# A mixture-of-experts layer on one core: another order of the 32 experts, and one norm of the last stage issued one tile later

## The chip, the core and the metric

The kernel runs on one core of one Trainium2 chip. Times are device microseconds (us) of that core for one whole launch. A core has TensorE (PE, matmuls and transposes; its weight loads are listed as PEld), VectorE (DVE), ScalarE (ACT), GpSimd (POOL) and SyncE (SP, which here only issues DMAs). Each engine works through its own queue in order, and they wait for one another by semaphores.

## The reference

One decoder layer on 1024 tokens of 1024 columns: a mixer (pooling and dilated attention), then a mixture of experts, a gated per-layer embedding and a final norm. What matters here:

```
h = rmsnorm(x);  logits = h @ w_router + b_router          # 32 experts, top 4 of each token
for each expert e, over the tokens that chose it:
    g, u = split(h @ w_gate_up[e] + b_gate_up[e])          # 1024 -> 2 x 1024
    a = (clip(u) + 1) * min(g, 7) * sigmoid(1.702 * min(g, 7))
    x[token] += gate * (a @ w_down[e] + b_down[e])
x += (p @ w_ple_proj) * sigmoid(rmsnorm(x) @ w_ple_gate)   # last stage, p: 1024 x 256
out = rmsnorm(x)
```

All of it is float32. The order in which the experts are taken is free.

## The kernel before, in words

**Exact products.** A float32 operand is split into a high and a low part (`split`, L103 to L105): ACT copies the high part (L104, tiles `wh`, `xh`, `ah`, `xr`), DVE subtracts it from the source (L105, `wl`, `xl`, `al`, `atr`). A product is then three matmuls (`mm3`, L98 to L101). Each half of a weight chunk of 128 x 2048 goes through this: one ACT instruction, then one DVE instruction.

**Places.** The experts are sorted by how many rows they have. The 18 largest (`N_MORE`, ranks 0 to 17) get 128 main rows and 32 *further* rows, the other 14 get 128. `processing_order` (L39) says which rank stands at which of the 32 places, `RANK` keeps it, and `REM[s]` is 1 where the expert at place `s` has further rows. This is a table made before the launch: it decides the order of instructions on every engine. Written as a string of `REM`, the table before is `01010101101010110101010110101011`.

**Main loop** (from L1177). The chunks are g(0), g(1), d(0), g(2), d(1), ... , g(31), d(30), d(31): g(s) is gate/up of place s (8 chunks), d(s) its down product (4 chunks). SP loads chunks six ahead into 7 tiles `raw`; ACT and DVE split them two chunks ahead of PE (`split_half`). The row groups below count a *window* from the first bias matmul of g(s) (L1029) to that of g(s+1); it holds g(s) and d(s-1). Beside the chunks a window has: the swiglu (`act_all`), the transposes of the result (`a_main`, L1007), the transposes of the next expert's rows (`x_main`), the row lists of place s+2 (`onehots`, `lists`) and, on POOL, gathers of rows (L934) and adds of results to `acc` in device memory (L1118).

**Further rows.** Where `REM[s]` is 1: `gu_rem` (L1043) puts 32 matmuls (L1057) after chunk k = 1 and 32 after k = 5 of g(s); `act_rem` is a small swiglu at k = 6; `x_rem(s)` (L1024, tile `xr`) transposes the gathered further rows during g(s-1), after its chunk k = 5 (PE L1019, then an ACT copy L1021); `a_rem` transposes the result (tile `atr`), `down_rem` (L1107) puts 64 matmuls (L1114) after chunk 1 of d(s) (after chunk 0 at the last place), and `y_rem` scales and adds (L1130, L1118).

**Last stage.** `proj(i)` (L1329), i = 0 to 7, multiplies tile i of p; its operand is transposed and split two tiles ahead (`turn_p`, L1170, PE L1174, ACT and DVE into `xr` and `atr`), and the products are copied out by ACT (L1336) and DVE (L1337). Into these eight steps the first norms of the stage are put: `early(n)` (L1390) squares tile n of the residual on ACT (L1346) and has nine small DVE instructions (`small_rsqrt`, L131 to L141) and one big one (L1349). `TURN0` (L1138) gives the values of i after which `early(0)` and `early(1)` are issued. Before `proj(7)` PE transposes the result of `early(0)` (`turn(0)`, L1007). Then come eight tiles of gate product, sigmoid, norm and store.

Of the kernel before, what the change touches and what calls it, by code (L numbers as in the profile page):

```python
# [26 lines left out]
NE = 32  # L27
# [7 lines left out]
N_MORE = 18  # L35
# [2 lines left out]

def processing_order():  # L39
    more, less = list(range(N_MORE)), list(range(N_MORE, NE))  # L40
    return [(more if (s + 1) * N_MORE // NE > s * N_MORE // NE else less).pop(0) for s in range(NE)]


RANK = processing_order()
REM = [int(r < N_MORE) for r in RANK]

# [25 lines left out]
def layer(ctx, tc, x, p, g_mix, w_in, w_pool, pool_scale, rel_bias, w_out, g_ffn, w_router,  # L72
# [170 lines left out]
    for i in range(NT):  # L243
# [13 lines left out]
        if i == 4:  # L257
            m = qk0.tile([128, 4, T], F32R, name="qk0")
            m = [m[:, 0], m[:, 1]]
# [257 lines left out]
    for u in range(32 + LAG + 2):  # L517
# [9 lines left out]
        if u == MIX:  # L527
            m = tbp.tile([128, 2, NK, 128], F32R, name="tb", bufs=1)
# [364 lines left out]
    def load_chunk(c, after=None, columns=slice(0, 2048)):  # L893
        kind, s, k = chunks[c]
        if c not in raws:
            raws[c] = wp.tile([128, 2048], F32, name="raw", bufs=7)
        if after is not None:
            after.memset(raws[c][:, columns][:, :1], 0.0)
        if kind in "jp":
            src = w_ple_gate[k * 256:(k + 1) * 256, :] if kind == "p" else w_ple_proj  # L900
            sp.dma_start(raws[c].rearrange("p (k c) -> p k c", k=2), src.rearrange("(k p) c -> p k c", p=128))
            return
        if s not in expert:
            expert[s] = sp.value_load(order[0:1, s:s + 1], min_val=0, max_val=NE - 1)
        e = expert[s]
        if kind == "g":
            sp.dma_start(raws[c][:, columns],
                         w_gate_up[ds(e, 1), k * 128:(k + 1) * 128, columns].rearrange("a p c -> p (a c)"))
        else:
            sp.dma_start(raws[c].rearrange("p (k c) -> p k c", k=2),  # L910
                         w_down[ds(e, 1), k * 256:(k + 1) * 256, :].rearrange("a (k p) c -> p (a k) c", p=128))
# [223 lines left out]
        y_rem(s)  # L1135
        S[s].clear()

    LOADS, SPLITS, TURN0, AT = 6, 4, (3, 7), 8  # L1138
    load_chunk(0, columns=slice(1024, 2048))

    lists(0, gates=False)
# [35 lines left out]
    for c, (kind, s, k) in enumerate(chunks[:nmain]):  # L1177
# [7 lines left out]
        if kind == "g":  # L1185
# [19 lines left out]
            if s == 0 and k == GK:  # L1205
                m = psM.tile([128, 2, 2, 6], F32, name="m", bufs=1)
# [241 lines left out]
```

## Time and profile before

| | |
|---|---|
| median of 3 runs | 1970.8 us (1970.47 to 1974.77) |
| profiled execution, its own time | 1971.62 us |
| its span, first to last instruction | 1969.8 us |
| PE busy | 1920.4 us (97%) |
| DVE, ACT, POOL busy | 1501.4, 1187.4, 282.0 us |
| main loop and last stage | from about 465 us to the end |

The busy time of PE counts a matmul from its start to its modelled end, and matmuls overlap: a matmul of 512 columns is shown with 0.39 us, but one starts every 0.227 us. So the loss of PE is read from the distance of two starts, or from the length of a window, not from the busy share.

### The profile page before, as it was taken

The page shows a single profiled execution, that of the slowest core. Times are in us where ns is not written, and L with a number is a line of the kernel's source. Part 1 is how long each engine was busy: PE and PEld are TensorE (multiplying, and loading weights), DVE is VectorE, ACT ScalarE, POOL GpSimd, SP SyncE. Part 2 cuts the span into 40 slices and gives each one's busy share as a digit, 9 for nine tenths or more (in the row PEclk, how much of TensorE's full clock was granted, in tenths as well). Part 3 has the DMA queues.
Part 4 walks back from the last instruction along what each step waited for, and adds up shares of the span by engine and source line. Part 5 has one row for each costly group of instructions (what it writes and reads, how often), then busy time and mean ns, then how long its engine had stood idle before and what let it go on. Part 6 is the DMA issues. An engine that isn't in the chain of part 4 may idle for free. (4 is left out here: it accounts for less than half of the span.)

```text
span 1969.8 us, 30297 instructions
## 1 busy us (share of the span) xinstructions
PE 1920.4 (97%) x11180; PEld 1428.8 (73%) x11181; DVE 1501.4 (76%) x2500; ACT 1187.4 (60%) x1706; POOL 282.0 (14%) x219
## 2 busy tenths in 40 slices
PE   7999999997999999999999999999999999999998
PEld 6778767775677776677776677776766777766786
DVE  5342575768889897888897888897977898978676
ACT  4221565445667676676676666776766676765533
POOL 0000121002122020212021212120202120201100
PEclk9999999997999999999999999999999999999999
DMA  4331212428889798798897798897987897987611
GB/s 150 115 93 38 87 45 65 137 110 316 345 319 354 282 378 306 285 345 340 310 363 283 294 349 328 311 360 279 359 322 291 317 353 283 377 308 275 205 65 54
DMA packets 117369, 502.18 MB, mean 255 GB/s; under 512 B 12560, under 2 KB 28944, under 8 KB 84576
## 3 DMA queue, kind: packets, MB, share of 16 engines
q1 hardware_dynamic: 99920, 451.46, 58.6%
q0 software_dynamic: 12960, 39.33, 8.5%
q10 hardware_dynamic: 4336, 9.40, 1.5%
q8 instruction: 89, 1.46, 0.3%
q14 instruction: 64, 0.52, 0.1%
HBM read 466.04 MB, written 38.83 MB: 256 GB/s over the span
## 5 line engine op out<-in xcount | busy, mean ns | idle before, releaser
L105 DVE TENSOR_TENSOR wl<-raw,wh 128x1024 fp32r<-128x1024 f32 x778 | 902.7, 1221 | 89.9 <-ACT wh L104 85.3
L104 ACT ACTIVATE wh<-raw 128x1024 fp32r<-128x1024 f32 x778 | 758.5, 1059 | 1.6 <-DMA raw<-in_w_gate_up 1.1
L99 PE MATMUL gu<-wh,xh 128*128 128x512 f32 x1152 | 487.3, 423 | 0.0
L100 PE MATMUL gu<-wl,xh 128*128 128x512 f32 x1152 | 449.7, 390 | 1.4 <-DVE wl L105 1.4
L101 PE MATMUL gu<-wh,xl 128*128 128x512 f32 x1152 | 449.9, 391 | 0.0
L99 PEld LDWEIGHTS gu<-wh,xh 128*128 128x128 f32 x1152 | 218.5, 190 | 47.8 <-issue 12.8
L101 PEld LDWEIGHTS gu<-wh,xl 128*128 128x128 f32 x1152 | 216.6, 188 | 46.5
L100 PEld LDWEIGHTS gu<-wl,xh 128*128 128x128 f32 x1152 | 217.7, 189 | 41.4 <-DVE wl L105 2.6
L100 PE MATMUL d<-wl,ah 128*128 128x512 f32 x512 | 199.9, 390 | 2.9 <-DVE wl L105 2.9
L99 PE MATMUL d<-wh,ah 128*128 128x512 f32 x512 | 201.6, 394 | 0.7 <-DVE al L105 0.7
L101 PE MATMUL d<-wh,al 128*128 128x512 f32 x512 | 199.2, 389 | 0.0
L1118 POOL DMA_INDIRECT acc<-y,idx x32 | 128.6, 4017 | 441.3 <-ACT y L1124 324.0
L934 POOL DMA_INDIRECT xg<-h2d,idx x32 | 52.7, 1645 | 671.4 <-PE gu L100 471.3
L1057 PE MATMUL r<-raw,xr 128*32 128x512 f32 x1152 | 130.5, 594 | 0.0
L1124 ACT ACTIVATE y<-d,gate 128x512 f32<-128x512 f32 x64 | 43.7, 689 | 127.1 <-PE d L101 122.4
L104 ACT ACTIVATE ah<-d 128x512 fp32r<-128x512 f32 x64 | 34.8, 596 | 139.4 <-PE d L1007 139.4
L105 DVE TENSOR_TENSOR al<-d,ah 128x512 fp32r<-128x512 f32 x64 | 41.2, 686 | 99.5 <-ACT ah L104 99.5
L99 PEld LDWEIGHTS d<-wh,ah 128*128 128x128 f32 x512 | 96.1, 188 | 27.8 <-ACT wh L104 7.0
L100 PEld LDWEIGHTS d<-wl,ah 128*128 128x128 f32 x512 | 96.1, 188 | 23.6 <-DVE wl L105 4.6
L101 PEld LDWEIGHTS d<-wh,al 128*128 128x128 f32 x512 | 96.1, 188 | 20.1
L104 ACT ACTIVATE xh<-d 128x512 fp32r<-128x512 f32 x80 | 43.7, 597 | 84.1 <-PE d L1007 84.1
L1057 PEld LDWEIGHTS r<-raw,xr 128*32 128x32 f32 x1152 | 34.2, 109 | 73.7 <-issue 72.1
(362 smaller groups left out, 2518.3 us busy)
## 6 DMA issues: line engine op xcount, KB each, us to landing
raw<-in_w_gate_up SPq DMA_DIRECT2D x255, 1024.0 KB, 5.8
raw<-in_w_down SPq DMA_DIRECT2D x128, 1024.0 KB, 5.4
wr<-in_w_in SPq DMA_DIRECT2D x16, 512.0 KB, 6.3
rrep<-rvec ACTq DMA_DIRECT2D x8, 576.0 KB, 13.9
xt<-in_x SPq DMA_DIRECT2D x8, 512.0 KB, 3.6
tb<-rrep SPq DMA_DIRECT2D x8, 512.0 KB, 6.1
wor<-in_w_out SPq DMA_DIRECT2D x8, 512.0 KB, 3.8
xr<-in_x SPq DMA_DIRECT2D x8, 512.0 KB
```

The costliest lines, as they stand in the source:

```text
L99: pe.matmul(ps, wh, xh, start=start, stop=False)
L100: pe.matmul(ps, wh, xl, start=False, stop=False)
L101: pe.matmul(ps, wl, xh, start=False, stop=stop)
L104: act.activation(hi, src, AF.Copy)
L105: dve.tensor_tensor(lo, src, hi.bitcast(F32), OP.subtract)
L934: pool.indirect_dma_start(out=xg, out_offset=None, in_=h2d4 if b else h2d, in_offset=bass.IndirectOffsetOnAxis(ap=S[s]["idx", b][:, :1], a ...
L1057: pe.matmul(S[s]["gur"][32 * j:32 * j + 32, :], S[s]["xr"][:, kk, :], raw[:, :, j, :], start=False, stop=(kk == NK - 1))
L1118: pool.indirect_dma_start(out=dst, out_offset=bass.IndirectOffsetOnAxis(ap=idx[:, :1], axis=0), in_=src, in_offset=None, compute_op=OP.add)
L1124: act.activation(y[:, 512 * b:512 * b + 512], S[s]["d"][b], AF.Copy, scale=S[s]["gate", 0])
```

## The change

The places are filled in another way: the first and the last place get an expert without further rows, and the 18 with further rows are spread over the 30 places between. The table is now `01010110101101011010110101101010`. Both tables have 18 ones and no two zeros side by side; they differ in the places where two ones meet: before at 7/8, 14/15, 23/24 and 30/31, now at 5/6, 10/11, 15/16, 20/21 and 25/26. The first place had no further rows before either. The second edit puts `early(0)` after `proj(4)` instead of `proj(3)`. Three lines more make every later line number larger by 3.

```diff
 def processing_order():
     more, less = list(range(N_MORE)), list(range(N_MORE, NE))
-    return [(more if (s + 1) * N_MORE // NE > s * N_MORE // NE else less).pop(0) for s in range(NE)]
+
+    n = NE - 2
+    many = [False] + [(s * N_MORE + n // 2) // n > ((s - 1) * N_MORE + n // 2) // n for s in range(1, n + 1)] + [False]
+    return [(more if m else less).pop(0) for m in many]
...
-    LOADS, SPLITS, TURN0, AT = 6, 4, (3, 7), 8
+    LOADS, SPLITS, TURN0, AT = 6, 4, (4, 7), 8
```

ACT in g(5), before: after the splits of the next expert's rows (`xh`) there are weight splits (`wh`), the small swiglu of place 5 (`uc`, `sg` from `r`) and the big one (from `gu`).

```order
L104 ACTIVATE xh<-d_6622 128x512
L104 ACTIVATE xh<-d_6629 128x512
L104 ACTIVATE wh<-raw 128x1024 x4
L1067 ACTIVATE uc_6706<-r 128x256
L1068 ACTIVATE sg<-r 128x256
L104 ACTIVATE wh<-raw 128x1024 x2
L1067 ACTIVATE uc_6773<-gu_6464 128x512
```

The same stretch of ACT now:

```order
L107 ACTIVATE xh<-d_6641 128x512
L107 ACTIVATE xh<-d_6648 128x512
L107 ACTIVATE wh<-raw 128x1024 x2
L1024 ACTIVATE xr<-m 128x2x4x32
L107 ACTIVATE wh<-raw 128x1024 x2
L1070 ACTIVATE uc_6730<-r 128x256
L1071 ACTIVATE sg<-r 128x256
L107 ACTIVATE wh<-raw 128x1024 x2
L1070 ACTIVATE uc_6778<-gu_6483 128x512
```

Place 6 now has further rows, so the copy of their transposes (`xr<-m`) stands in front of two weight splits and of the swiglu. Before, such a copy stood inside the window of an expert with further rows at places 7, 14, 23 and 30.

PE around the start of d(31), the down product of the last place, before: the last matmul of d(30), the transposes of the swiglu's result (`uc512`), those of the further rows (`uc256`), and the first matmuls of d(31).

```order
L101 MATMUL d1_17730<-wh_17749,al_17530 128x512
L1007 MATMUL d0_17853<-ident_62,uc512_17706 128x128 x4
L1007 MATMUL d1_17860<-ident_62,uc512_17710 128x128 x4
L1019 MATMUL m_17867<-ident_62,uc256_17677 128x128 x2
L99 MATMUL d0_17882<-wh_17800,ah_17851 128x512
L100 MATMUL d0_17882<-wl_17801,ah_17851 128x512
```

The same place on PE now:

```order
L104 MATMUL d1_17771<-wh_17790,al_17594 128x512
L1010 MATMUL d0_17894<-ident_62,uc512_17747 128x128 x4
L1010 MATMUL d1_17901<-ident_62,uc512_17751 128x128 x4
L102 MATMUL d0_17918<-wh_17841,ah_17892 128x512
L103 MATMUL d0_17918<-wl_17842,ah_17892 128x512
```

The two transposes of the further rows are gone from here, and so are the 64 matmuls (L1114) that stood after the first chunk of d(31); both kinds now stand in windows of earlier places.

DVE between `proj(3)` and `proj(5)`, before: the end of `early(0)` (`nr`, `y`), then the low part of tile 6 of p (`atr`), the copy out of `proj(4)`, a weight split, and the low part of tile 7.

```order
L141 SCALAR_TENSOR_TENSOR nr_18380<-na_18382,nr_18380 128x1
L1349 SCALAR_TENSOR_TENSOR y_18375<-xg_18260,nr_18380,oh_18257 128x1024
L105 TENSOR_TENSOR atr_18404<-m_18405,xr_18403 128x256
L1337 COPY raw_18390<-gu1_18254 128x512
L105 TENSOR_TENSOR wl_18413<-raw_17932,wh_18412 128x1024
L105 TENSOR_TENSOR atr_18429<-r_18430,xr_18428 128x256
```

DVE now: the low part of tile 6 (`atr_18388`), the copy and the split come first, and then `early(0)` begins.

```order
L108 TENSOR_TENSOR atr_18388<-m_18389,xr_18387 128x256
L1340 COPY raw_18374<-gu1_18254 128x512
L108 TENSOR_TENSOR wl_18397<-raw_17932,wh_18396 128x1024
L1396 TENSOR_SCALAR ss2_18400<-ss2_18400 128x1
L134 TENSOR_SCALAR nn_18404<-ss2_18400 128x1
L136 TENSOR_SCALAR nr_18406<-nn_18404 128x1
```

The whole of `early(0)` moved behind three instructions; it now stands ahead of the low part of tile 7 instead of tile 6.

## Rows read from the trace of the kernel before

**Rows 1.** The page: busy time of PE, and TensorE's clock in 40 slices.
```profile
PE 1920.4 (97%) x11180; PEld 1428.8 (73%) x11181; DVE 1501.4 (76%) x2500; ACT 1187.4 (60%) x1706; POOL 282.0 (14%) x219
...
PEclk9999999997999999999999999999999999999999
```

**Rows 2.** Waits of PE: line, releaser, us in total, times, longest.
```profile
PE d L100 <- DVE wl L105: 2.9, 4, 0.8
...
PE gu L101 <- DVE atr L105: 0.7, 1, 0.7
PE d L99 <- DVE al L105: 0.7, 1, 0.7
```

**Rows 3.** Windows of places 5 to 9: length, then busy time of each engine, PEclk, DMA.
```profile
663.54:707.22 43.68, 43.68 (x250) 30.87 (x250) 34.81 (x54) 29.46 (x38) 6.24 (x4) 1.00 0.85 313
707.22:747.52 40.30, 40.30 (x250) 31.35 (x250) 38.03 (x54) 29.10 (x37) 10.19 (x3) 1.00 0.90 350
747.52:792.23 44.71, 43.96 (x243) 30.76 (x243) 33.64 (x48) 29.52 (x39) 4.46 (x3) 1.00 0.84 316
792.23:839.98 47.75, 47.75 (x316) 32.91 (x316) 39.55 (x58) 29.48 (x38) 10.44 (x3) 1.00 0.77 282
839.98:880.10 40.12, 40.12 (x242) 31.16 (x242) 35.10 (x47) 29.47 (x38) 4.46 (x3) 1.00 0.91 345
```

**Rows 4.** Timeline of PE in d(6) and d(29): start us, us, instruction [idle before].
```profile
785.72 0.39 PE L99 MATMUL d<-wh,ah 128*128 128x512 f32 x1
786.86 0.50 PE L100 MATMUL d<-wl,ah 128*128 128x512 f32 x1 [0.75 <-DVE wl L105]
...
1770.20 0.39 PE L99 MATMUL d<-wh,ah 128*128 128x512 f32 x1
1771.22 0.50 PE L100 MATMUL d<-wl,ah 128*128 128x512 f32 x1 [0.62 <-DVE wl L105]
```

**Rows 5.** Timeline of ACT in the window of place 7.
```profile
774.69 0.39 ACT L1021 ACTIVATE xr<-m 128x256 f32<-128x256 f32 x1 [4.13 <-PE m L1019]
...
781.25 7.70 ACT L104 ACTIVATE wh<-raw 128x1024 fp32r<-128x1024 f32 x8
```

**Rows 6.** Timeline of DVE in the same window.
```profile
785.59 4.63 DVE L105 TENSOR_TENSOR wl<-raw,wh 128x1024 fp32r<-128x1024 f32 x4
```

**Rows 7.** Timeline of PE at the start of d(31).
```profile
1824.30 0.38 PE L1019 MATMUL m<-ident,uc 128*128 128x128 f32 x2
1825.38 0.50 PE L99 MATMUL d<-wh,ah 128*128 128x512 f32 x1 [0.70 <-DVE al L105]
...
1828.01 0.39 PE L101 MATMUL d<-wh,al 128*128 128x512 f32 x1
...
1831.91 0.50 PE L99 MATMUL d<-wh,ah 128*128 128x512 f32 x1
```

**Rows 8.** Timeline of PE in `proj(6)` and at `turn(0)`.
```profile
1859.56 0.39 PE L100 MATMUL gu<-wl,xr 128*128 128x512 f32 x1
1860.70 0.50 PE L101 MATMUL gu<-wh,atr 128*128 128x512 f32 x1 [0.75 <-DVE atr L105]
...
1863.10 1.04 PE L1007 MATMUL d<-ident,y 128*128 128x128 f32 x8
```

**Rows 9.** Timeline of ACT around `early(0)` and `proj(4)`.
```profile
1855.73 1.06 ACT L1346 ACTIVATE y<-xg 128x1024 f32<-128x1024 f32 x1 [0.37 <-issue]
...
1857.53 1.06 ACT L104 ACTIVATE wh<-raw 128x1024 fp32r<-128x1024 f32 x1
```

**Rows 10.** Timeline of DVE in `early(0)`: its first and last instruction, and the next.
```profile
1856.92 0.15 DVE L1393 TENSOR_SCALAR ss<-ss 128x1 f32<-128x1 f32 x1 [0.30 <-ACT y L1346]
...
1859.02 1.29 DVE L1349 SCALAR_TENSOR_TENSOR y<-xg,nr,oh 128x1024 f32<-128x1024 f32 x1 [0.22 <-DVE nr L141]
1860.22 0.42 DVE L105 TENSOR_TENSOR atr<-m,xr 128x256 fp32r<-128x256 f32 x1
```

**Rows 11.** A stretch before the main loop, columns as in rows 3.
```profile
447.50:468.00 20.50, 13.44 (x68) 8.71 (x67) 14.51 (x56) 10.24 (x19) 2.18 (x8) 0.50 0.62 227
```

## The prediction, made before the changed kernel was run

> **What bounds the kernel now.** I read the page's busy rows first: PE is busy 97% of the span, and its clock row stands near full throughout [rows 1]. A busy share proves little, since overlapping matmuls are counted whole, so I went to the list of PE's waits next. It is short: from the main loop on, the entries are 2.9 us in four waits for `wl`, 0.7 us in one for `al` and 0.7 us in one for `atr` [rows 2]; nothing there waits for a weight load. Then I cut the main loop into windows from one expert's first bias matmul to the next one's. The reader should see that a window's length depends only on who has further rows, and that PE's busy time equals the length except in one of the five [rows 3]. So the order cannot make the stream shorter; both orders have the same number of matmuls. It can only add or remove gaps of PE, and move work into or out of gaps. The sum below counts these.
>
> **The windows by kind.** Write a window as (place before, own place, next place, the one after). The trace shows (0,1,0,1) at 43.68 us, (1,0,1,1) at 40.30, (0,1,1,0) at 44.71, (1,1,0,1) at 47.75 and (1,0,1,0) at 40.12 [rows 3]; all the other windows of places 2 to 29 repeat one of these within 0.02 us. Before, places 2 to 29 hold 9 windows of 43.68, 9 of 40.12, 4 of 40.30, 3 of 44.71 and 3 of 47.75: 393.12 + 361.08 + 161.20 + 134.13 + 143.25 = 1192.8 us. With the new table they hold 6, 7, 5, 5 and 5: 262.08 + 280.84 + 201.50 + 223.55 + 238.75 = 1206.7 us, which is 13.9 more. Every window of the new table is of a kind that the trace has, with the same neighbours two places to either side. This is why I trust the sum.
>
> **What leaves the end in return.** At the last place an expert with further rows is replaced by one without. Three pieces go.
> - In the window of place 30: the two transposes of place 31's further rows and the gap described below. An (0,1,1,0) window is 44.71 against 43.68 of (0,1,0,1), which is 1.03; the fourth gap is 0.13 shorter than the others and a list of place s+2 with further rows costs 0.18 (40.30 less 40.12), so I put this at 1.06.
> - In the window of place 31: its further gate/up matmuls. From 47.75 less 40.12, corrected by the same 0.18 and by the 0.30 for the transposes (1.03 + 0.18 - 0.91), that is 7.75.
> - In d(31): the 64 further matmuls, from the matmul at 1828.01 to the one at 1831.91 less one step of 0.23: 3.67 [rows 7].
>
> The loop's sum is +13.9 - 1.06 - 7.75 - 3.67 = **+1.4 us**, slower. Two causes stand behind it, and they can be priced alone:
>
> 1. *One more pair.* Where an expert with further rows is followed by another, PE has a gap: from 785.72 to 786.86 is 1.14 us against a step of 0.23, so 0.91 is lost; in the fourth such pair it is 1.02, so 0.79 [rows 4]. The chain behind it: in g(7) ACT must copy the transposes of place 8's further rows, but PE reaches them only after the 32 further matmuls of place 7, and ACT sits idle 4.13 us [rows 5]. That eats its lead; the swiglu follows, the next weight splits start at 781.25 [rows 5], and DVE's `wl` starts at 785.59 [rows 6], just too late. Where only one of the neighbours has further rows the window has no such gap. There were 4 pairs, there are 5: 5 x 0.91 - (3 x 0.91 + 0.79) = +1.03.
> 2. *A cover lost.* At the start of d(31) PE waits for `al` in any case [rows 2, 7]. The two transposes of the last expert's further rows (1824.30) ran inside this wait; now all eighteen such pairs run in the full stream. The full cost of further down rows in a window is 47.75 - 43.68 = 4.07, at the last place 3.67: +0.4.
>
> Bounds for the pairs: below, no gap at any pair in the new spacing, -3.5 instead of +1.0; above, twice the gap in each pair after the first. I take the measured gap, since three of four agree to 0.01 us.
>
> **The norm, one tile later.** Before, `early(0)` holds DVE from 1856.92 to 1860.31, and the low part of tile 6 stands behind it [rows 10]; PE waits for that part in `proj(6)`: 1859.56 to 1860.70 is 1.14, so 0.91 lost [rows 8]. With `early(0)` behind the copy and the split of `proj(4)` this gap goes. What is late next is `turn(0)`, which needs the norm's result. ACT's last work in `proj(4)` is the split at 1857.53, ending at 1858.59 with the squares in front of it and up to 0.3 earlier without [rows 9]. From the start of the squares to DVE's first instruction of the norm it is 1.19 (1855.73 to 1856.92) [rows 9, 10], plus at most the 0.37 of idle time that stood ahead of the squares: DVE begins between 1859.5 and 1860.1. The DVE work of the norm takes 3.39 (1856.92 to 1860.31) [rows 10], so the result is there between 1862.9 and 1863.5, and `turn(0)` starts some 0.06 later. Before, it started at 1863.10, the gap included; without it PE would be there at 1862.19 [rows 8]. So PE waits 0.8 to 1.4 us at `turn(0)` instead of 0.91 in `proj(6)`: -0.1 to +0.5, and I take +0.1. The low part of tile 7 is now behind the norm on DVE, done 0.4 after it, while PE still has 0.8 us of transposes: covered. The copy out of `proj(5)` is one more 0.7 us later, needed only when `proj(7)` reaches its second half. The residual tile itself comes no later than before, because POOL no longer has the add of the last place's further rows ahead of the last big add; with the norm a tile later that gain has nothing to shorten. From `turn(0)` on PE has no gap worth a term until the last tile, and the end is the same program.
>
> **Sum.** +1.4 and +0.1 make +1.5 us. The profiled execution took 1971.62 (span 1969.8 and 1.8 around it), so that run would become 1973.1. It lies 0.8 above the median of the runs; on the median of 1970.8 the forecast is **1972.3 us**, 0.08% more. Differences under 0.2%, here 3.9 us, cannot be told from none.
>
> **A rule that speaks against the change.** In all five windows, the one with the gap of 0.91 included, the granted clock is 1.00, the level of 2.4 GHz [rows 3]; from 447.5 to 468 with PE busy 13.44 of 20.50 us, it was 0.50, the level of 1.2 GHz [rows 11]. The Trainium skill says in "TensorE: Matmul & The Clock Gate", section "Why this matters for your kernels", that idle gaps between bursts of matmuls bring the engine back to half rate. By the rows a gap of 0.91 does not do that here; by the rule alone a longer one would, and the fourth rival takes its time from the rows.
>
> **Rivals.**
> - *The norm's gap goes and none takes its place* (squares and DVE chain start earlier than I think): +1.4 - 0.9 = +0.5, 1971.3 us. For it: only 0.8 us are to be found. Against it: the chain of 3.39 cannot start before the split's DVE half is done.
> - *The pairs lose their gap* in the new spacing: -3.5 and +0.4 and +0.1, about 1967.8; with the first rival too, 1966.9. Against it: the window of a pair depends on nothing that the spacing changes.
> - *The slower end: pairs five places apart do not recover.* ACT's and DVE's lead of two chunks would have to be lost at one pair and not be back at the next, so that the gap doubles from the second pair on: 4 x 0.91 = 3.7 more, 1976.0. It decides from the point where the windows after a pair are longer than 40.12; the trace speaks against it, since the first window after the pair has exactly this length and no PE gap [rows 3].
> - *The clock falls at one of the gaps* (the longest is that at `turn(0)`), and PE runs at the lower level for some 20 us as it did from 447.5 to 468 [rows 11]: half of 20.5 is lost, about +10, 1982. Against it: gaps of this size before left the clock at 1.00.
>
> **How the numbers follow.** Forecast 0.78, first rival 0.09, second 0.05, third 0.06, clock 0.02. The forecast's own range is 1971 to 1974; single runs of the kernel before lie between 1970.47 and 1974.77, and the bounds of the pairs reach from 1967.8 to 1976.0. I give 1968.8 to 1976.0. Faster by over 0.2% (below 1966.9) needs the second rival with the first, or a shift of the measurement: 0.04. Slower by over 0.2% (above 1974.7) takes the third and the clock, and a little of the forecast's scatter: 0.08. The rest, 0.88, is within.
>
> **What would show it.** In the changed profile PE should have a gap of about 0.9 us before `wl` at five places, in d(4), d(9), d(14), d(19) and d(24), and none in d(29); windows of 44.7 and 47.7 us at places 5/6, 10/11, 15/16, 20/21 and 25/26; no wait for `atr` in `proj(6)` and one for `y` at `turn(0)`; the wait before d(31) without the small transposes in it, and the next matmul at the same distance from the end of d(30). I would be wrong if a window after a pair is longer than 40.2 us, if PE's waits list a DMA in the main loop, or if the clock row shows a new fall.

## The result: 10 us slower, and where they went

The changed kernel takes 1981.94 us (median of 5 runs, 1980.06 to 1983.29), the kernel before 1971.56 (5 runs): ratio 1.0051, 95% interval 1.004 to 1.0061. That is above the forecast of 1972.3 and outside the range. The profiled execution took 1981.48, its span is 1979.7, 9.9 longer than before. (Lines of the changed kernel carry numbers 3 higher than before.)

The page hardly shows it; the rows answer to [rows 1]:

```profile
PE 1921.4 (97%) x11180; PEld 1429.4 (72%) x11181; DVE 1500.7 (76%) x2500; ACT 1187.1 (60%) x1706; POOL 271.9 (14%) x219
...
PEclk9999999998999999999999999999999999999999
```

PE is again 97% busy, and no slice of the clock row has fallen, since one slice is 49 us. PE's list of waits does show it (line, releaser, us in total, times, longest), against [rows 2]:

```profile
PE m L1177 <- SPq L1239: 7.0, 1, 7.0
...
PE d L103 <- DVE wl L108: 4.1, 5, 1.1
```

The second row is the forecast five pairs, and there is no wait for `atr` any more. The first row is new: one wait of 7.0 us at line 1177, the first transpose of `turn_p(0)`, which turns the input `p`. The releaser in such a row is inferred; what PE waits for here is the tile of `p`: its last packet ended at 1842.41, and PE went on 0.33 us later. PE's timeline around it (start us, us, instruction [idle before]):

```profile
1835.35 0.39 PE L104 MATMUL d<-wh,al 128*128 128x512 f32 x1
1842.74 0.69 PE L1177 MATMUL m<-ident,raw 128*128 128x128 f32 x2 [7.01 <-SPq L1239]
1843.08 0.78 PE L102 MATMUL d<-wh,ah 128*128 128x512 f32 x1
1843.66 0.63 PE L103 MATMUL d<-wl,ah 128*128 128x512 f32 x1
1844.08 0.63 PE L104 MATMUL d<-wh,al 128*128 128x512 f32 x1
...
1847.01 0.40 PE L102 MATMUL d<-wh,ah 128*128 128x512 f32 x1
1847.24 0.39 PE L103 MATMUL d<-wl,ah 128*128 128x512 f32 x1
```

Behind the wait the matmuls start 0.43 us apart instead of 0.23 and last 0.63 instead of 0.39, until 1847. The windows of the same stretch give the clock (columns as in [rows 3]):

```profile
1835.35:1842.74 7.39, 0.39 (x2) 0.00 (x0) 0.00 (x0) 0.00 (x0) 1.55 (x1) 0.82 1.04 339
1842.74:1847.01 4.27, 4.27 (x12) 3.46 (x13) 2.60 (x3) 2.27 (x3) 0.00 (x0) 0.51 0.06 10
1847.01:1851.28 4.27, 3.82 (x19) 2.83 (x17) 0.61 (x2) 0.66 (x2) 0.00 (x0) 1.00 0.01 4
```

After 7.0 us without a matmul the granted clock is 0.51, the level of 1.2 GHz, then 1.00 again. The first row also has the cause in it: while PE waits, the DMA engines are busy throughout (1.04). So `p` was not late in being asked for; its bytes were late in coming. The DMA queues while `p`'s packets ran, before and then after (packets, MB, share of 16 engines; q10 is ACT's queue and carries `p`, q1 is SP's with the weights):

```profile
q1 hardware_dynamic: 349, 1.30, 46.1%
q10 hardware_dynamic: 1040, 1.05, 43.5%
```

```profile
q1 hardware_dynamic: 1179, 4.51, 66.7%
q0 software_dynamic: 204, 0.59, 18.4%
q10 hardware_dynamic: 1040, 1.05, 17.6%
```

The first window is 1821 to 1828, the second 1825.5 to 1842.5. `p` is 1 MB in packets of 1 KB, the weights come in packets of 4 KB. Before, `p` needed 6.5 us, with SP's queue empty from 1825.9 to 1830.6. After, it needed 16.8, and in that time 1040 packets of `p` went beside 1179 of SP's queue, so `p` got 1.05 of 6.15 MB. Two cuts of the second window show the sharing best: 1827 to 1833, and 1834 to 1838, where an add of POOL to `acc` (q0) runs as well:

```profile
q1 hardware_dynamic: 495, 1.92, 78.6%
q10 hardware_dynamic: 493, 0.50, 23.9%
```

```profile
q0 software_dynamic: 125, 0.50, 62.0%
q1 hardware_dynamic: 128, 0.52, 33.9%
q10 hardware_dynamic: 128, 0.13, 9.2%
```

The queues go packet for packet. So `p` moves 82 packets in a microsecond beside one other queue and 32 beside two; in the trace before, it moved 373 in the microsecond from 1825.5, next to alone. POOL's add thus has a part in the delay, by these rates some 2.4 us (an estimate: 4 us at 32 instead of 82). The Trainium skill says in "DMA: Bandwidth & Descriptors", section "Queues, rings and completion order", that each DMA engine goes round the queues that have work, a packet at a time; the trace agrees with its 493 beside 495. No run gave `p` larger packets, so what that would bring is not shown.

Why SP's queue was empty before and full after is in SP's issues (start us, us, instruction), before and then after:

```profile
1815.70 0.38 SPq L901 DMA_DIRECT2D raw<-in_w_ple_proj  x1
1816.56 15.85 SPq L901 DMA_DIRECT2D raw<-in_w_ple_gate  x4
```

```profile
1820.30 0.38 SPq L904 DMA_DIRECT2D raw<-in_w_ple_proj  x1
1821.16 12.27 SPq L904 DMA_DIRECT2D raw<-in_w_ple_gate  x4
```

`p` is issued 0.87 us behind the first gate load in both (at 1817.43 and 1822.03). The three gate loads behind it go out from 1829.45 on before, 12.9 us after the first, and from 1823.19 on after, 2.0 us after the first. SP's waits in these stretches (1805 to 1845 before, 1810 to 1850 after) say what held it:

```profile
SPq L901 <- PE r L1114: 13.3, 5, 10.8
```

```profile
SPq L904 <- DVE wl L108: 10.5, 3, 7.1
```

Before, SP waited up to 10.8 us for line 1114, the further matmuls in d(31), which read four `raw` tiles straight from the buffer; the next loads need those tiles. With no further rows at the last place nobody reads the tiles after the weight splits, the buffers come free earlier, and 3 MB of weights run beside `p`. Landing of a gate load went from 5.9 us (median) to 10.6.

The spans' difference by stages:

| stage | predicted | measured |
|---|---|---|
| main loop to place 31's first bias matmul | +12.88 | +13.00 |
| g(31) and d(30) | -7.75 | -7.71 |
| entry to d(31), and d(31) to `turn_p(0)` | -3.67 | -3.78 |
| wait at `turn_p(0)` (7.39 less a step of 0.23) | none | +7.16 |
| low clock, `turn_p(0)` to the tenth matmul behind it (4.27 less 2.29) | none | +1.98 |
| `proj(0)` to `turn(0)` (21.64 against 21.75) | +0.1 | -0.11 |
| the rest, nearly all of it ahead of the main loop | 0 | -0.69 |
| sum | +1.5 | +9.9 |

### The profile page after: what moved, and what is told of

Its sections match the earlier page's. It is cut to its first block, busy times and chain, and to the rows that moved or that the text cites. A ratio compares the mean times of both kernels' runs of the same rounds, so it can differ in the third digit from the quotient of the medians.

```text
span 1979.7 us, 30291 instructions
## 1 busy us (share of the span) xinstructions
PE 1921.4 (97%) x11180; PEld 1429.4 (72%) x11181; DVE 1500.7 (76%) x2500; ACT 1187.1 (60%) x1706; POOL 271.9 (14%) x219
## 5 line engine op out<-in xcount | busy, mean ns | idle before, releaser
L1121 POOL DMA_INDIRECT acc<-y,idx x32 | 118.4, 3701 | 448.8 <-ACT y L1127 378.5
```

The costliest lines, as they stand in the source:

```text
L1121: pool.indirect_dma_start(out=dst, out_offset=bass.IndirectOffsetOnAxis(ap=idx[:, :1], axis=0), in_=src, in_offset=None, compute_op=OP.add)
```

## The experiments

My theory (A): the freed tiles start loads that collide with `p`; the wait costs 7, the clock 2. The rivals: the later norm has a part, the order of the other 31 places has one, or the wait comes from the issue of `p` and not from its neighbours.

**The order alone.** The changed kernel with the norm where it was:

```diff
-    LOADS, SPLITS, TURN0, AT = 6, 4, (4, 7), 8
+    LOADS, SPLITS, TURN0, AT = 6, 4, (3, 7), 8
```

Expected:

> The new table of places with the norm where it was (after proj(3)). Theory A (load): at the last place no further matmuls hold the weight tiles any more, so three gate loads of the last stage run beside the load of p, p lands late and PE waits some 7 us at the first transposes of p, with a fall of the clock behind it. The norm has no part in it: 1981.9 us, +-0.6, the same 7 us wait. Rival N (norm): the moved norm is what costs: about 1972 us, no such wait.

Measured: 1982.76 us (1979.48 to 1985.21, 4 runs), ratio 1.0062 (1.0046 to 1.0077). PE's waits have that row again, with 6.0 us in the profiled execution, the fastest of the four:

```profile
PE m L1177 <- SPq L1239: 6.0, 1, 6.0
```

The loss is there without the later norm.

**`p` on SP's queue.** The changed kernel with one word changed, so that `p` goes behind the first gate load and ahead of the other three, in one queue:

```diff
-                act.dma_start(pall, p.rearrange("(i t) c -> t i c", t=128))
+                sp.dma_start(pall, p.rearrange("(i t) c -> t i c", t=128))
```

Expected:

> The changed kernel with the load of p issued from SP, between the first and the second gate load, so that it stands ahead of the other three in the same queue. Theory A: p lands before PE needs it, no wait, no fall of the clock: 1981.9 - 9.3 = 1972.6 us, which is the sum of the prediction. Rival Q (p's own load is slow: 1024 packets of 1 KB, asked for too late for a shorter last down product, whatever runs beside it): the wait stays within 1 to 2 us of 7, about 1981.

Measured: 1972.84 us (1971.98 to 1973.86, 11 runs), ratio 1.0006 (0.9997 to 1.0015). PE's timeline at `turn_p(0)`:

```profile
1835.82 0.40 PE L104 MATMUL d<-wh,al 128*128 128x512 f32 x1
1836.05 0.38 PE L1177 MATMUL m<-ident,raw 128*128 128x128 f32 x2
1836.19 0.47 PE L102 MATMUL d<-wh,ah 128*128 128x512 f32 x1
```

No wait and no low clock: 9.1 us come back and the five pairs stay. The time is 1.4 above that of the kernel before, measured beside it (1971.45), where my sum said 1.5; 1.4 cannot be told from none. All of the loss lies in how `p` shares the DMA engines.

**The last place's down product left out of the kernel before.** Here the old order stays and only the holder of the four tiles goes: the last place's further down product, its scaling and its add are left out (their result is missing from the output).

```diff
-        if not REM[s] or kp != (s < NE - 1):
+        if not REM[s] or s == NE - 1 or kp != (s < NE - 1):
...
-            if s == NE - 1 and k == 0:
-                y_rem(s)
```

Expected:

> The kernel before, its order and norm untouched, with the further down product of the last place left out (64 matmuls, their scaling and their add). Theory A: the weight tiles come free earlier, p's load shares the DMA engines with three gate loads and takes some 17 us instead of 6.5; PE comes 3.7 us earlier and waits 5 to 7 us, with some 2 us for the clock: 1971.6 - 3.7 + 6 + 2 = 1976 us. Rival Q, and any theory that blames the order of the other 31 places: p lands as before, 7 us ahead of need; no wait, 1971.6 - 3.7 = 1967.9 us.

Measured: 1976.17 us (1974.48 to 1979.05), ratio 1.0022 (1.0012 to 1.0031). PE's timeline, then the queues from 1821 to 1838:

```profile
1830.56 0.39 PE L101 MATMUL d<-wh,al 128*128 128x512 f32 x1
1837.96 0.66 PE L1174 MATMUL m<-ident,raw 128*128 128x128 f32 x2 [7.01 <-SPq L1234]
```

```profile
q1 hardware_dynamic: 1153, 4.40, 65.4%
q0 software_dynamic: 218, 0.60, 19.4%
q10 hardware_dynamic: 1032, 1.04, 17.4%
```

Taking 3.7 us of PE's work away made the kernel 4.7 us slower than the kernel before (1971.45), with the very wait of 7.01. Its second gate load goes out 2.0 us after the first, as in the changed kernel. The order of the other 31 places is not to blame: what matters is who holds the tiles.

**The three gate loads held back.** The changed kernel, with the last three gate loads issued behind a small write of DVE that follows the split of `p`'s first tile:

```diff
-        if c + LOADS < len(chunks):
+        if c + LOADS < nmain + 2:
...
+                if k == 1:
+                    for n in range(nmain + 2, nmain + 5):
+                        load_chunk(n, after=dve)
```

Expected:

> The changed kernel, p's load left on ACT's queue, but the last three gate loads may start only when the first tile of p has been split. Theory A: p's load takes about 6.5 us as before the change, no wait at its transposes: 1972.6 us (more, if a late gate load then holds up the splits of the last stage, up to 1975). Rival Q: the wait of some 7 us stays, 1981 to 1982.

Measured: 1976.99 us (1975.44 to 1979.82), ratio 1.0028 (1.0018 to 1.0038). `p`'s packets ran 7.3 us (1825.8 to 1833.2) and the wait at line 1177 is gone, but PE has two new waits in the last stage:

```profile
q10 hardware_dynamic: 1040, 1.05, 40.2%
```

```profile
PE gu L102 <- ACT raw L1342: 2.8, 1, 2.8
...
PE gu L104 <- DVE atr L108: 0.8, 1, 0.8
```

It shows the collision from the other side: without the three loads beside it, `p` is hardly delayed. The median lies 2 above the 1975 that the expectation allowed; the two rows account for 3.6 of the 4.2 between this kernel and the one with `p` on SP's queue. ACT, which the first of them waits for, stands still until 1849.30 ahead of the last place's `y`, for 9.73 us against 4.35 there; that the late loads hold it is likely, but not shown.

**The wait filled with useless matmuls.** To price the clock alone, 32 matmuls whose result nobody reads stand ahead of `turn_p(0)` in the changed kernel:

```diff
+                if k == 1:
+                    t = psM.tile([128, 512], F32, name="gu3", bufs=1)
+                    for n in range(32):
+                        pe.matmul(t, S[s]["ad"][0][:, 0, :], parts[2 * c][0][:, :512], start=True, stop=True)
```

Expected:

> The changed kernel with 32 matmuls of no use (512 columns, 0.227 us apart, 7.3 us in all, into a PSUM bank that is free) put on PE ahead of the first transposes of p, so that PE works through the wait for p. It parts the cost of the wait from that of the clock. Theory A: PE finds p there within 0.5 us, the clock stays at 1.00, and the time is that of the changed kernel less the slow stretch, 1981.9 - 2.1 = 1979.8 us. Rival: the fall of the clock costs nothing by itself, 1981.9 us.

Measured: 1980.29 us (1979.96 to 1980.7), ratio 1.0039 (1.0024 to 1.0054), 1.65 under the changed kernel, though single runs of the two overlap. Windows over the stretch and behind it:

```profile
1835.00:1843.00 8.00, 8.00 (x37) 6.58 (x36) 0.48 (x1) 0.00 (x0) 1.55 (x1) 1.00 1.03 329
1843.00:1848.00 5.00, 5.00 (x25) 4.11 (x24) 3.12 (x4) 2.66 (x4) 0.00 (x0) 1.00 0.04 8
```

The clock stays at 1.00. `p`'s last packet ended at 1841.95, and the transpose starts at 1843.04, straight behind the useless matmuls, so here they set its start and not `p`. From that transpose to the end it is 135.16 us, in the changed kernel 136.96: the low clock costs 1.80, by the table above 1.98. The wait itself is the other 7. These matmuls are as useless as the wait, and PE's busy share would hide the loss.

**The norm early, with `p` on SP's queue.** The same word changed as above, and `TURN0` back at (3, 7). Expected:

> The new order with p loaded from SP, and the norm back after proj(3): against the same kernel with the norm after proj(4) (1972.84 us) it prices the second edit alone. By the prediction the gap before proj(6) comes back (0.91) and the wait at turn(0) goes (0.87 in the changed kernel): 1972.9 us, +-0.5. Rival: the later norm is worth its whole gap, 1973.7 us.

Measured: 1973.54 us (1971.67 to 1978.21, 11 runs), ratio 1.0008 (0.9999 to 1.0017): by time not told apart from 1972.84. In the profile `proj(0)` to `turn(0)` takes 21.36 us, against 21.65 with the norm late and 21.75 before; the gap in `proj(6)` comes back with 0.5 instead of 0.91. Three other traces with the early norm agree: 21.37 (the order alone), 21.40 (the last down product left out) and 21.34 (the kernel before with its transposes early, below). Two of these have the old order, so it is not the new order that shortens this stretch. In the trace of the kernel before ACT stood still for 0.37 us ahead of the squares [rows 9], in none of these four; why is open. By the traces the second edit costs some 0.3 us.

**The pair's gap removed, in either kernel.** The prediction's first cause rests on ACT copying the transposes of the next expert's further rows too late. So they are made one chunk earlier, once in the kernel before, once in the changed one with `p` on SP's queue:

```diff
                 if k == 4:
                     x_main(s + 1)
-                if k == 5:
                     x_rem(s + 1)
```

Expected:

> The kernel before, with the transposes of the next expert's further rows one chunk earlier (after chunk 4 instead of 5), so ahead of the 32 further matmuls of the present expert. Theory (prediction's reading of the pairs): ACT no longer waits 4 us for these transposes, the four gaps of 0.8 to 0.9 us go and nothing else moves: 1971.5 - 3.5 = 1968.0 us. Rival: the gap comes of the amount of work that a pair puts on ACT and DVE, not of the wait: it stays, 1971.5 us.

> The changed kernel with both: p loaded from SP, and the transposes of the next further rows one chunk earlier. Theory: no wait for p and no gap at the five pairs (5 x 0.91, one of them 1.27 in the profile): 1972.8 - 4.9 = 1967.9 us, level with the same edit on the order before (1968.0), so that the order itself is worth nothing either way. Rival: the new order is worth more once both are out of the way, below 1967 us.

Measured: 1968.23 us (1966.76 to 1969.92, 10 runs), ratio 0.9979 (0.997 to 0.9988), and 1967.93 (1967.3 to 1969.21, 9 runs), ratio 0.9978 (0.9968 to 0.9988). Place 7 of the first, against 44.71 in [rows 3]:

```profile
747.05:790.77 43.72, 43.72 (x243) 30.89 (x242) 34.56 (x49) 29.73 (x39) 4.46 (x3) 1.00 0.83 309
```

The length is now PE's busy time, and no `d` wait for `wl` is left in either. Four gaps of about 0.9 gave 3.6 us; five gave 4.9 against 1972.84. The main loops of the traces are 3.66 and 4.83 shorter. Both beat the kernel before and the changed one, and they stand level: with the pair's gap and the collision out of the way the order of the experts is worth nothing measurable.

## Why the prediction was wrong

- **What bounds the kernel, and the windows by kind: right.** The sum over the loop missed by 0.1. The windows of places 5 to 7 after are of the forecast kinds, 44.7, 47.7 and 40.1:

```profile
662.95:707.64 44.69, 43.93 (x243) 30.76 (x243) 33.62 (x48) 29.52 (x39) 4.48 (x3) 1.00 0.85 318
707.64:755.38 47.74, 47.74 (x315) 32.89 (x315) 39.54 (x58) 29.48 (x38) 10.46 (x3) 1.00 0.77 281
755.38:795.48 40.10, 40.10 (x241) 31.15 (x241) 35.04 (x47) 29.45 (x38) 5.41 (x3) 1.00 0.91 343
```

- **One more pair: right, and shown**, since moving the transposes took the gaps away. Four of the five gaps are 0.91 or 0.92; that at place 20 is 1.27, which I had not foreseen.
- **A cover lost, +0.4: right** in its place (-3.78 for -3.67), seen in the first rows of d(31) after, against [rows 7]: the wait for `al` is there without the small transposes.

```profile
1827.72 1.33 PE L1010 MATMUL d<-ident,uc 128*128 128x128 f32 x8
1829.98 0.50 PE L102 MATMUL d<-wh,ah 128*128 128x512 f32 x1 [0.92 <-DVE al L108]
```

- **The norm: right to 0.2.** The gap in `proj(6)` is gone and PE waits for `y` at `turn(0)`, against [rows 8]. The row's 0.72 is 0.87 in my measure (from start to start, less a step of 0.23), where I said 0.8 to 1.4. Against the one trace of the kernel before, the stretch is 0.11 shorter; by the other traces with an early norm it is 0.3 longer, where I said 0.1.

```profile
1871.82 0.39 PE L104 MATMUL gu<-wh,atr 128*128 128x512 f32 x1
1872.92 1.09 PE L1010 MATMUL d<-ident,y 128*128 128x128 f32 x8 [0.72 <-DVE y L1352]
```

- **"In d(31): the 64 further matmuls ... 3.67": the step that failed.** The 3.67 was right as PE's time. But I priced the removed matmuls as PE's work only. They also held four weight tiles, and the wait that they put on SP (13.3 us in five waits) kept the last three gate loads out of its queue until `p` had come. `p` had no term in the sum, neither its landing nor its 1 KB packets. "Nothing there waits for a weight load" was true of PE before and no reason for after: the margin of a load is not in the list of waits at all. Before, `p`'s packets ended at 1827.63 and PE took up `turn_p(0)` at 1834.77: 7.1 us to spare. The shorter d(31) takes 3.8 of that, the collision 10.3 (16.8 less 6.5), and 10.3 + 3.8 - 7.1 = 7.0 is the wait, within 0.2.
- **"The clock falls at one of the gaps": the right number by luck.** That rival stood at 1982, with the fall at `turn(0)` and 20 us of low clock; 1981.94 was measured. The clock did fall, but 30 us earlier (1842.74 against 1872.92), behind a wait that the rival did not know of, and the fall alone costs 2. Its price of 10 was too high in any case: PE is busy for 13.44 of the 20.50 us in [rows 11], so a halved clock can lose no more than 6.7 there. Of the signs of being wrong that I had named, the clock row shows none, since its slices are too long; the list of waits shows one, with SP's queue named, in d(31). By "TensorE: Matmul & The Clock Gate", section "Why this matters for your kernels", of the Trainium skill, idle gaps between bursts of matmuls bring half rate. Here 7.01 us did (0.51), while windows with gaps of 0.9 kept 1.00.
- **The slower end, pairs that do not recover: no.** The window after the pair is 40.10.

## What to carry to other kernels

An instruction that is taken away or moved also stops holding its buffers: ask which loads wait for them, when those will start now, and which transfer in another queue they will run beside. For each load near the place, write down its landing and its first reader in the profile before, since a load with slack shows up in no list of waits. Here the urgent transfer did better ahead of the big loads in their own queue than in a queue to itself, by 9.1 us.

## What the hardware showed that I had not expected

- A 1 MB load of 1 KB packets went packet for packet with the queues beside it (493 to 495; 128 to 128 and 125), so it got about a sixth of the bytes (1.05 of 6.15 MB) and took 16.8 us instead of 6.5, though it had a queue to itself. In the queue of the weights, ahead of three of them, it was in time.
- Behind a wait of 7.0 us the clock stood at 0.51; with the wait filled by matmuls it stayed at 1.00. One such fall cost 1.8 to 2.0 us.
- Taking away 3.7 us of work on the busiest engine cost 4.7 us.
